# The last two gate column blocks as one group of products, with the first token half ahead

## The chip, the cores and the metric

The kernel runs on one core of a Trainium2 chip. The metric is the device time of one execution in microseconds (us); of several runs the median is taken. Engines: PE (TensorE, matmul; PEld is its weight load), DVE (VectorE), ACT (ScalarE), POOL (GpSimd), SP (SyncE, which issues nearly all transfers).

## The reference

One layer over 256 tokens of width 4096, in float32. Two branches (chunked attention and a convolution module) give `y`; then come the residual sum, a gate and a final norm. The change is in the gate and the norm.

```python
h = h + jnp.concatenate([y_a, y_c], axis=-1) @ w_out[i]
gate = jax.nn.sigmoid(rms_norm(h, ple_norm_g[i]) @ w_ple_gate[i] + b_ple_gate[i])
h = h + gate * (p[i] @ w_ple[i])
return rms_norm(h, final_g)
```

`w_ple_gate` is 4096 x 4096, `w_ple` 256 x 4096. The final norm needs the sum of squares of a whole row of `h`, so no output can be stored before the last column block is done for its tokens.

## The kernel before

**Numbers in two parts.** A matmul in full float32 is made of three in the format fp32r: each operand is split into a high part (`wh`, a cast on ACT, L197) and a low part (`wl`, the remainder, a subtraction on DVE, L198); the kinds are high x high, low x high, high x low. The tokens are two halves of 128 (`h` is 0 or 1), the 4096 output columns eight blocks of 512 (`c` is 0 to 7), the 4096 input columns 32 k-blocks of 128.

**Two ways to multiply.** `product` (matmuls at L210, in `accumulate`) takes one column block: for each k-block six matmuls of 128x512, three kinds for two token halves. `mixed_product` (matmuls at L351, in `add`) takes two column blocks at once: a pair of k-blocks, two column blocks and two token halves form a 2x2 by 2x2 block product. A plain pair is eight products, 24 matmuls. A pair with a star in the order list is done by seven products (Winograd's form of Strassen's method), 21 matmuls; for that DVE adds weight tiles (`ua`, `ub`, L398 to L403), and the sums are split as well (`uh`, `ul`). Four more PSUM banks (`P1`, `P5`, `P6`, `P7`) hold helper products, which `helper_sums` folds into the tiles `z` when the last starred pair is done.

**Order.** `units` turns a text into the order of the 16 pairs, with stars. A scheduler orders the instructions of each engine; what is marked by `pin` keeps the program's order. `later` is a queue of small steps, of which `fill` takes a few after each pair. The pool `w` has five buffers for weight tiles as loaded, `wh` and `wl` three each, `uh` and `ul` two; SP issues a load when a buffer is released.

**The gate.** `gated_pair` does the blocks 0 to 5 in three groups of two: `mixed_product` over `w_ple_gate`, then the embedding `p @ w_ple` by `product` into `pacc` (24 matmuls), then the gate: multiply-add (L978), sigmoid (L979), and by way of `later` the product with `pacc`, the sum into `hc`, the sum of squares (`square_sum`, L469) and the product with the final weight (L177).

**The last two blocks.** Blocks 6 and 7 go by `product`, one after the other; block 7 with `lag`: the last six weight tiles (of two k-blocks each) are kept, four of them in big tiles, and used for the first token half alone. So its sum is ready first: `add_gated` (L927 to L932) and `finish` (the mean at L473 and L125, the power at L126, scalings at L941 to L945, stores at L946) run for it while `rest` does the 36 matmuls of the second half. Then `add_gated` and `finish` follow for that.

```python
acc, rest = product(w_ple_gate[0], c * NB, hT, KD, lag=lag)
add_gated(c, 0, acc[0], pacc[0], row, fg)
rest()
finish(0, fg)
add_gated(c, 1, acc[1], pacc[1], row, fg)
finish(1, fg)
```

Of the kernel before, what the change touches and what calls it, by code (L numbers as in the profile page):

```python
# [10 lines left out]
F32 = mybir.dt.float32  # L11
F32R = mybir.dt.float32r
AF = mybir.ActivationFunctionType
# [3 lines left out]
P = 128  # L17
NB = 512
# [8 lines left out]
def hybrid_block(  # L27
# [107 lines left out]
    def big_tile(pool=None):  # L135
        return (pool or big).tile([P, 4, 2, T], F32R, tag="big", name="big_t")
# [64 lines left out]
        )  # L201
        return (wh, wl), made

    def accumulate(acc, h, lhs, kb, wh, wl, k, kblocks, kinds=range(3)):
        t, i = lhs[kb // 4], kb % 4
        xh = t[:, i, 0, h * P : (h + 1) * P]
        xl = t[:, i, 1, h * P : (h + 1) * P]
        for kind in kinds:
            a, b = ((xh, wh), (xl, wh), (xh, wl))[kind]
            nc.tensor.matmul(  # L210
                acc, a, b[:, k, :],
                start=kb == 0 and kind == 0, stop=kb == kblocks - 1 and kind == 2,
            )

    def product(w, col, lhs, kblocks, pool=None, tag="acc", ahead=None, lag=(), given=(), fills=2):

        acc = [
            (pool or ps_acc).tile([P, NB], F32, tag=tag, name=f"acc{h}") for h in range(NH)  # L220
        ]
        starts = list(range(len(given))) + list(range(len(given), kblocks, KC))
        kept = starts[len(starts) - len(lag) :] if lag else []
        held = []
        for k0 in starts:
            kc = 1 if k0 < len(given) else min(KC, kblocks - k0)
            if k0 < len(given):
                wh, wl = given[k0]
                for kind in range(3):
                    for h in range(NH):  # L230
                        accumulate(acc[h], h, lhs, k0, wh, wl, 0, kblocks, (kind,))
                continue
            keep = k0 in kept
            wh, wl = weight_parts(w, col, k0, kc, lag[kept.index(k0)] if keep else None)
            if keep:
                held.append((k0, kc, wh, wl))
            for k in range(kc):
                for h in range(1 if keep else NH):
                    accumulate(acc[h], h, lhs, k0 + k, wh, wl, k, kblocks)
                if ahead and given and k0 + k == len(given):  # L240
                    ahead(k0)
            if ahead:
                ahead(k0 + kc)
            fill(fills)

        def rest():
            for k0, kc, wh, wl in held:
                for k in range(kc):
                    accumulate(acc[1], 1, lhs, k0 + k, wh, wl, k, kblocks)

        return (acc, rest) if lag else acc

# [66 lines left out]
    def units(text):  # L321

        return [(int(u.rstrip("*")), u.endswith("*")) for u in text.split()]
# [3 lines left out]
    dense = units("1 0* 3 2* 5 4* 6* 7 8* 9 10* 11 12* 14* 13 15")  # L327
    delayed = units("1 3 5 7 0* 9 2* 11 4* 13 6* 15 8* 10 12 14")
    early = units("1 3 5 7 0* 9 2* 11 4* 13 6* 15 8 10 12 14")
    late = units("1 3 5 7 9 11 13 15 0* 2 4* 6 8* 10* 12 14")  # L330

    def mixed_product(
        w, col, lhs, comb, order, on_helpers, ahead=None, fills=0, on_begin=None, apart=NB
    ):

        c = [[ps_acc.tile([P, NB], F32, tag="acc", name=f"acc{h}{j}") for j in range(2)] for h in range(NH)]
        helper = {}
        begun, ends = set(), {}  # L340
        for n, (_, seven) in enumerate(order):
            for name in ("P1", "P5", "P6", "P7", "P2", "P3", "P4") if seven else ("P2", "P3", "P4", "X"):
                ends[name] = n
        banks = {"P2": c[0][0], "P3": c[0][1], "P4": c[1][0], "X": c[1][1]}
        made = []

        def add(name, x, w2, n, final):

            for kind, (a, b) in enumerate(((x[0], w2[0]), (x[1], w2[0]), (x[0], w2[1]))):
                made.append(  # L350
                    nc.tensor.matmul(  # L351
                        banks[name], a, b, start=name not in begun,
                        stop=final and ends[name] == n and kind == 2,
                    )
                )
                begun.add(name)
# [6 lines left out]
        for n, (pair, seven) in enumerate(order):  # L363
# [3 lines left out]
            for k in range(2):  # L367
                wt = wpool.tile([P, 2, NB], F32, tag="w", name="wt")
                kb = 2 * pair + k
                rows = w[kb * P : (kb + 1) * P, :]  # L370
                nc.sync.dma_start(
                    wt,
                    bass.AP(
                        tensor=rows.tensor, offset=rows.offset + col,
                        ap=[list(rows.ap[0]), [apart, 2], [1, NB]],
                    ),
                )
                wts.append(wt)
            if not seven:
                for k in range(2):  # L380
                    wh, wl = parts_of(wts[k], 2)[0]
                    for j in range(2):
                        for h in range(NH):
                            name = (("P2", "P3"), ("P4", "X"))[h][j]
                            add(name, block(2 * pair + k, h), (wh[:, j], wl[:, j]), n, k == 1)
                fill(fills)
                continue
# [39 lines left out]
            if n == last_seven:  # L427
                on_helpers(helper)
            fill(fills)
        return c  # L430

    tt, stt = nc.vector.tensor_tensor, nc.vector.scalar_tensor_tensor
    QUARTERS = ((0, 0), (1, 0), (0, 1), (1, 1))
# [30 lines left out]
            )  # L464
        return t

    def square_sum(dst, src):
        junk = spool.tile([P, NB], mybir.dt.bfloat16, tag="junk", name="junk", bufs=1)
        nc.scalar.activation(junk, src, AF.Square, accum_out=dst)  # L469

    def rstd_of(partial, n, name):
        r = cpool.tile([P, partial.shape[1]], F32, name=name)
# [447 lines left out]


    n_f = D // NB
    ssq_f = cpool.tile([P, NH, n_f], F32, name="ssq_f")

    def add_gated(c, h, acc, pacc, row, fg):
        hc, gt = hs[c][:, h, :], gts[h]
        nc.vector.scalar_tensor_tensor(gt, acc, r_h[:, h : h + 1], row, ALU.mult, ALU.add)  # L927
        nc.scalar.activation(gt, gt, AF.Sigmoid)
        nc.vector.tensor_tensor(gt, pacc, gt, ALU.mult)
        last = c == n_f - 1  # L930
        (nc.vector if last else nc.gpsimd).tensor_tensor(hc, hc, gt, ALU.add)
        square_sum(ssq_f[:, h, c : c + 1], hc)  # L932
        if not last:
            nc.gpsimd.tensor_tensor(hc, hc, fg, ALU.mult)

    def finish(h, fg):
        r = rstd_of(ssq_f[:, h : h + 1, :], D, f"r_f{h}")
        for c in range(n_f - 1, -1, -1):
            hc = hs[c][:, h, :]
            if c == n_f - 1:  # L940
                nc.vector.scalar_tensor_tensor(hc, hc, r, fg, ALU.mult, ALU.mult)  # L941
            elif c % 2:
                nc.vector.tensor_scalar(hc, hc, r, None, ALU.mult)
            else:
                nc.scalar.activation(hc, hc, AF.Identity, scale=r)  # L945
            nc.sync.dma_start(out[0, h * P : (h + 1) * P, c * NB : (c + 1) * NB], hc)  # L946

    def gated_pair(c0, order, ahead):

# [26 lines left out]
        for h, j in QUARTERS:  # L976
            gt, hc = z[h][j], hs[c0 + j][:, h, :]
            stt(gt, acc[h][j], r_h[:, h : h + 1], gt, ALU.mult, ALU.subtract if j else ALU.add)  # L978
            nc.scalar.activation(gt, gt, AF.Sigmoid)  # L979
            later.append(partial(tt, gt, pacc[j][h], gt, ALU.mult))  # L980
            todo.append(partial(tt, hc, hc, gt, ALU.add))
            todo.append(partial(square_sum, ssq_f[:, h, c0 + j : c0 + j + 1], hc))
            todo.append(partial(tt, hc, hc, fgs[j], ALU.mult))
        later.extend(todo)

    for c0 in range(0, n_f - 2, 2):
        gated_pair(c0, steady if c0 else late, None if c0 else h_ahead)

    for c in range(n_f - 2, n_f):
        row = broadcast_row(b_ple_gate, c * NB, NB)  # L990
        fg = broadcast_row(final_g, c * NB, NB)
        pacc = product(w_ple[0], c * NB, pT, PLE // P, pool=ps_tmp, tag="tmp")
        gt = spool.tile([P, NH, NB], F32, tag="stage", name="gt")
        gts = [gt[:, h, :] for h in range(NH)]
        if c < n_f - 1:
            acc = product(w_ple_gate[0], c * NB, hT, KD)
            for h in range(NH):
                add_gated(c, h, acc[h], pacc[h], row, fg)
        else:
            keep = [big_tile(more).rearrange("q a b t -> q (a b t)") for _ in range(4)]  # L1000
            lag = [
                [t[:, i * KC * NB : (i + 1) * KC * NB].rearrange("q (k n) -> q k n", n=NB) for i in range(2)]
                for t in keep
            ] + [None] * 3
            acc, rest = product(w_ple_gate[0], c * NB, hT, KD, lag=lag)
            add_gated(c, 0, acc[0], pacc[0], row, fg)
            rest()
            finish(0, fg)
            add_gated(c, 1, acc[1], pacc[1], row, fg)
            finish(1, fg)  # L1010


# [28 lines left out]
```

## Time and profile before

| | |
|---|---|
| Median of 3 runs | 2061.18 us (2059.1 to 2062.29) |
| The profiled execution's own time | 2063.82 us |
| Its span | 2061.7 us |
| Mean granted TensorE clock | 0.996 |
| PE busy | 2034.6 us (99%) |
| DVE busy | 1822.1 us (88%) |
| ACT busy | 1152.9 us (56%) |

The profile is one execution; its span goes from the first to the last instruction, and its own time lies 2.1 us above. Lines with L are lines of the kernel before. In rows of instruction groups the operands stand as out<-in. In the stretches, each engine's busy us is followed by the number of its instructions. In the timeline, a bracket tells how long the engine had been idle and what released it.

### The profile page before, as it was taken

What the parts mean: (1) busy time and instruction counts of PE and PEld (TensorE: products, weight loads), DVE (VectorE), ACT (ScalarE), POOL (GpSimd) and SP (SyncE); (2) the same over time, 40 slices, a digit from 0 to 9 for tenths busy, and PEclk for the clock granted to TensorE, in tenths of its full rate; (3) what the DMA queues carried; (4) which work ended last, traced back from release to release, by engine and by line L of the source; (5) the groups of instructions that cost most, each with busy time, mean ns of one, the idle gap of its engine ahead of it and who ended that gap; (6) DMA issues with size and microseconds to landing.
All of it is one profiled execution on the core that took longest, in us unless ns stands there. A gap on an engine that the chain in (4) does not pass through costs nothing.

```text
span 2061.7 us, 25882 instructions
## 1 busy us (share of the span) xinstructions
PE 2034.6 (99%) x9140; PEld 1675.2 (81%) x9140; DVE 1822.1 (88%) x2541; ACT 1152.9 (56%) x1479; POOL 42.9 (2%) x37
## 2 busy tenths in 40 slices
PE   9999999999999999999999999999999999999997
PEld 7888888887888787788888888878888888888886
DVE  7599999899977998875889999899999999999954
ACT  7445535554564535575556656576565666656543
POOL 0000000000000002300000000000000000000000
PEclk9999999999999999999999999999999999999998
DMA  8656665656566665555666666666666656666664
GB/s 291 186 186 201 191 197 184 195 188 188 175 204 185 194 190 164 186 184 195 194 210 202 200 215 197 212 229 206 212 202 206 211 185 192 210 229 210 220 208 166
DMA packets 170331, 412.27 MB, mean 200 GB/s; under 512 B 13006, under 2 KB 16222, under 8 KB 170202
## 3 DMA queue, kind: packets, MB, share of 16 engines
q1 hardware_dynamic: 169914, 410.11, 62.5%
q8 instruction: 71, 1.16, 0.2%
q10 hardware_dynamic: 288, 0.52, 0.1%
q14 instruction: 58, 0.48, 0.1%
HBM read 406.39 MB, written 4.19 MB: 199 GB/s over the span
## 4 chain that ended last, share of the span: by engine, by line
PE 90%; DVE 6%; issue 2%; DMA 1%; ACT 1%; POOL 0%; SPq 0%; ACTq 0%; POOLq 0%; DVEq 0%
PE acc L351 53%; PE acc L210 22%; PE acc_P L351 13%; DVE wl L198 2%; DVE cv L574 1%; PE tmp_ps L156 1%; DVE ul L198 1%; DMA wt<-in_w_in_dram 1%; DMA wt<-in_w_ple_gate_dram 0%; PE tmp_ps L724 0%; PE tmp_ps L739 0%; PE tmp_ps L757 0%; ACT wh L197 0%; DMA xin<-in_x_dram 0%; PE tmp_ps L762 0%
## 5 line engine op out<-in xcount | busy, mean ns | idle before, releaser
L197 ACT CAST wh<-wt 128x1024 fp32r<-128x1024 f32 (+1 forms) x741 | 727.0, 991 | 628.8 <-PE acc L351 319.6
L351 PE MATMUL acc<-wh,big_t 128*128 128x512 f32 x3344 | 1038.8, 391 | 3.4 <-ACT big_t L142 2.9
L198 DVE TENSOR_TENSOR wl<-wt,wh 128x1024 fp32r<-128x1024 f32 (+1 forms) x741 | 850.7, 1159 | 130.2 <-ACT wh L197 127.6
L351 PEld LDWEIGHTS acc<-wh,big_t 128*128 128x128 f32 x3344 | 626.7, 188 | 133.3 <-ACT big_t L142 3.4
L351 PE MATMUL acc<-wl,big_t 128*128 128x512 f32 x1672 | 652.1, 391 | 3.3 <-DVE wl L198 3.2
L210 PE MATMUL acc<-wh,big_t 128*128 128x512 f32 x1248 | 390.2, 393 | 0.0
L351 PEld LDWEIGHTS acc<-wl,big_t 128*128 128x128 f32 x1672 | 314.4, 188 | 71.9 <-DVE wl L198 7.2
L210 PEld LDWEIGHTS acc<-wh,big_t 128*128 128x128 f32 x1248 | 234.9, 189 | 48.2 <-DVE big_t L143 0.2
L210 PE MATMUL acc<-wl,big_t 128*128 128x512 f32 x624 | 243.4, 391 | 0.0
L574 DVE SCALAR_TENSOR_TENSOR cv<-uT,dw,cv 128x256 f32<-128x256 f32 x480 | 214.3, 487 | 1.0
L197 ACT CAST uh<-ub 128x1024 fp32r<-128x1024 f32 x103 | 108.3, 1051 | 113.1 <-DVE ub L403 92.4
L351 PE MATMUL acc_P<-uh,big_t 128*128 128x512 f32 x534 | 163.7, 390 | 0.0
L197 ACT CAST uh<-ua 128x1024 fp32r<-128x1024 f32 x103 | 108.6, 1054 | 63.9 <-DVE ua L399 59.0
L210 PEld LDWEIGHTS acc<-wl,big_t 128*128 128x128 f32 x624 | 117.9, 189 | 24.1
L198 DVE TENSOR_TENSOR ul<-ub,uh 128x1024 fp32r<-128x1024 f32 x103 | 128.2, 1245 | 7.9 <-ACT uh L197 7.1
L198 DVE TENSOR_TENSOR ul<-ua,uh 128x1024 fp32r<-128x1024 f32 x103 | 125.8, 1222 | 0.4
L351 PEld LDWEIGHTS acc_P<-uh,big_t 128*128 128x128 f32 x534 | 99.9, 188 | 21.4 <-ACT uh L197 0.8
L351 PE MATMUL acc_P<-ul,big_t 128*128 128x512 f32 x267 | 103.8, 393 | 0.9 <-DVE ul L198 0.9
L398 DVE TENSOR_TENSOR ua<-wt 128x512 f32<-128x512 f32 x103 | 71.6, 695 | 30.7 <-DMA wt<-in_w_in_dram 17.4
L399 DVE TENSOR_TENSOR ua<-wt 128x512 f32<-128x512 f32 x103 | 70.8, 688 | 4.6 <-DMA wt<-in_w_in_dram 4.3
L403 DVE TENSOR_TENSOR ub<-ub,wt 128x512 f32<-128x512 f32 x103 | 72.2, 701 | 1.2
L402 DVE TENSOR_TENSOR ub<-ua,wt 128x512 f32<-128x512 f32 x103 | 70.9, 688 | 0.2
(199 smaller groups left out, 1349.3 us busy)
## 6 DMA issues: line engine op xcount, KB each, us to landing
wt<-in_w_in_dram SPq DMA_DIRECT2D x447, 512.0 KB, 3.9
wt<-in_w_out_dram SPq DMA_DIRECT2D x128, 512.0 KB, 4.2
wt<-in_w_ple_gate_dram SPq DMA_DIRECT2D x128, 512.0 KB, 4.0
wt<-in_w_pw_dram SPq DMA_DIRECT2D x32, 512.0 KB, 4.3
hc<-in_x_dram SPq DMA_DIRECT2D x8, 512.0 KB, 5.3
wt<-in_w_ple_dram SPq DMA_DIRECT2D x8, 512.0 KB, 4.7
out_dram<-hc SPq DMA_DIRECT2D x16, 256.0 KB, 2.9
xin<-in_x_dram SPq DMA_DIRECT2D x7, 512.0 KB, 8.3
```

The lines of the kernel that those rows point to most:

```text
L156: nc.tensor.transpose(pt[:, i * T + h * P : i * T + (h + 1) * P], src[:, h, b * P : (b + 1) * P], ident,)
L197: nc.scalar.copy(wh[:, :kc, :], wt[:, :kc, :]),
L198: nc.vector.tensor_tensor(wl[:, :kc, :], wt[:, :kc, :], wh[:, :kc, :].bitcast(F32), ALU.subtract),
L210: nc.tensor.matmul(acc, a, b[:, k, :], start=kb == 0 and kind == 0, stop=kb == kblocks - 1 and kind == 2,)
L351: nc.tensor.matmul(banks[name], a, b, start=name not in begun, stop=final and ends[name] == n and kind == 2,)
L398: plus(ua[:, 0], w0[:, 0], w0[:, 1])
L399: plus(ua[:, 1], w0[:, 1], w1[:, 1])
L402: plus(ub[:, 0], ua[:, 0], w1[:, 1])
L403: plus(ub[:, 1], ub[:, 0], w1[:, 0])
L574: nc.vector.scalar_tensor_tensor(cv[:, i, :], uT[:, i, k : k + T], dw[:, b, k : k + 1], cv[:, i, :], ALU.mult, ALU.add,)
```

## The change

The blocks 6 and 7 become one group of `mixed_product`, in the order `final`: 7 of the 16 pairs are starred. The last three pairs of that order (13, 14 and 15) are left out of the group's own loop: their weight tiles are split and held (the first three in `wh` and `wl`, the last three in big tiles), and `add_left` multiplies them later, first for token half 0 in both blocks, then for half 1 in block 6, and last for half 1 in block 7, there as two halves of 256 columns in banks of their own, 36 matmuls instead of 18.

The embedding of these blocks is done after the left products of each token half (`embedded`), with `uh` and `ul` for its weight parts. The gate, the sums and the final norm are pinned in a written order. The square is scaled so that the sum of squares is the mean, `EPS` is a column of `ssq_f`, and all but the last entry are summed ahead (`sum_of`), so that one small sum (`rstd_with`) and the power stay behind the last square. The outputs of the blocks 6 and 7 are multiplied by the final weight ahead of the scaling (`weigh`). `product` loses its `lag`.

```diff
+    final = units("1 0* 3 2* 5 4* 6* 7 8* 9 10* 12* 11 13 14 15")
...
+        n_left = len(left) // 2
-        for n, (_, seven) in enumerate(order):
+        for n, (_, seven) in enumerate(order[: len(order) - n_left]):
...
+        def add_left(h, js, out=None, cols=slice(None)):
+            for m in range(0, len(held), 2):
+                for j in js:
+                    dst = c[h][j] if out is None else out[:, cols]
+                    for i, (kb, (wh, wl)) in enumerate(held[m : m + 2]):
+                        xh, xl = block(kb, h)
+                        for kind, (a, b) in enumerate(((xh, wh), (xl, wh), (xh, wl))):
+                            pin(
+                                nc.tensor.matmul(
+                                    dst, a, b[:, j, cols],
+                                    start=out is not None and m + i + kind == 0,
+                                    stop=m + i + 1 == len(held) and kind == 2,
+                                )
+                            )
...
+            if n >= len(order) - n_left:
+                for k in range(2):
+                    tiles = left[2 * (n - len(order) + n_left) + k]
+                    held.append((2 * pair + k, parts_of(wts[k], 2, tiles and tiles())[0]))
+                fill(fills)
+                continue
...
-    ssq_f = cpool.tile([P, NH, n_f], F32, name="ssq_f")
+    ssq_f = cpool.tile([P, NH, n_f + 2], F32, name="ssq_f")
+    nc.vector.memset(ssq_f[:, :, :1], EPS)
+    square_f = partial(square_sum, scale=D ** -0.5)
...
+    acc, add_left = mixed_product(
+        w_ple_gate[0], c0 * NB, hT, hS, final, on_helpers, fills=4, on_begin=on_begin,
+        left=[None] * 3 + [kept] * 3,
+    )
+    fill(len(later))
+    w_p = []
+    for j in range(2):
+        wt = wpool.tile([P, 2, NB], F32, tag="w", name="wt")
+        nc.sync.dma_start(
+            wt, w_ple[0, :, (c0 + j) * NB : (c0 + j + 1) * NB].rearrange("(k q) n -> q k n", q=P)
+        )
+        w_p.append(pair_parts(wt))
...
+    def gate(h, j, a, op, cols=slice(0, NB)):
+        gt = z[h][j][:, cols]
+        pin(stt(gt, a, r_h[:, h : h + 1], gt, ALU.mult, op))
+        pin(nc.scalar.activation(gt, gt, AF.Sigmoid))
+
+    def add_gated(h, j, pacc, at, cols=slice(0, NB)):
+        gt, hc = z[h][j][:, cols], hs[c0 + j][:, h, cols]
+        pin(tt(gt, pacc[:, cols], gt, ALU.mult))
+        pin(tt(hc, hc, gt, ALU.add))
+        pin(square_f(ssq_f[:, h, at : at + 1], hc))
+
+    def weigh(h, j, cols=slice(0, NB)):
+        pin(tt(z[h][j][:, cols], hs[c0 + j][:, h, cols], fgs[j][:, cols], ALU.mult))
...
+    def store(h, r):
+        for c in range(n_f):
+            t = hs[c][:, h, :] if c < c0 else z[h][c - c0]
+            if c % 2:
+                pin(nc.scalar.activation(t, t, AF.Identity, scale=r))
+            else:
+                pin(nc.vector.tensor_scalar(t, t, r, None, ALU.mult))
+            nc.sync.dma_start(out[0, h * P : (h + 1) * P, c * NB : (c + 1) * NB], t)
+
+    pin(stt(z[1][1], acc[1][1], r_h[:, 1:2], z[1][1], ALU.mult, ALU.subtract))
+    add_left(0, range(2))
+    gate(0, 0, acc[0][0], ALU.add)
+    gate(0, 1, acc[0][1], ALU.subtract)
+    for j in range(2):
+        add_gated(0, j, embedded(0, j), n_f - 1 + j)
+    weigh(0, 0)
+    r = rstd_with(0, sum_of(0, n_f), n_f)
+    weigh(0, 1)
+    add_left(1, [0])
+    store(0, r)
+    gate(1, 0, acc[1][0], ALU.add)
+    paccs = [embedded(1, j) for j in range(2)]
+    add_gated(1, 0, paccs[0], n_f - 1)
+    weigh(1, 0)
+    halves = [slice(i * NB // 2, (i + 1) * NB // 2) for i in range(2)]
+    parts = []
+    for cols in halves:
+        parts.append(ps_acc.tile([P, NB], F32, tag="acc", name="part"))
+        add_left(1, [1], parts[-1], cols)
+    for i, cols in enumerate(halves):
+        gate(1, 1, parts[i][:, cols], ALU.add, cols)
+        if i:
+            weigh(1, 1, halves[0])
+        add_gated(1, 1, paccs[1], n_f + i, cols)
+    s = sum_of(1, n_f + 1)
+    weigh(1, 1, halves[1])
+    store(1, rstd_with(1, s, n_f + 1))
```

## The prediction

> **What bounds the kernel now.** I read the page's busy times first, then the stretches, the chain that ended last, DVE's waits, and the timeline of the last matmuls.
>
> ```profile
> PE 2034.6 (99%) x9140; PEld 1675.2 (81%) x9140; DVE 1822.1 (88%) x2541; ACT 1152.9 (56%) x1479; POOL 42.9 (2%) x37
> ...
> core 0: us, PE busy (x) PEld busy (x) DVE busy (x) ACT busy (x) POOL busy (x), PEclk, DMA share, GB/s
> 1866.00:1890.00 24.00, 24.00 (x107) 19.74 (x106) 23.90 (x32) 14.56 (x22) 0.00 (x0) 1.00 0.59 188
> 1980.00:1990.00 10.00, 10.00 (x46) 8.29 (x45) 4.30 (x4) 4.22 (x4) 0.00 (x0) 1.00 0.59 183
> ...
> 1939.97 10.43 PE acc L351 x46
> 1950.40 88.41 PE acc L210 x390
> ```
>
> PE is full in both stretches, but they differ. At 1866 (a group by `mixed_product`) DVE has 23.9 of 24 us too; at 1980 (column block 6 by `product`) DVE has 4.3 of 10. The chain gives the pace: 46 matmuls in 10.43 us, 0.2267 us each. So fewer matmuls shorten the last part only if DVE, idle there now, can make the operands of a seven-product group in time.
>
> ```profile
> DVE ua L398 <- DMA wt<-in_w_ple_gate_dram: 2.2, 1, 2.2
> DVE z L978 <- PE acc L351: 1.3, 1, 1.3
> DVE ul L198 <- ACT uh L197: 1.2, 1, 1.2
> ...
> 1808.14 2.36 DVE L198 TENSOR_TENSOR wl<-wt,wh 128x1024 fp32r<-128x1024 f32 x2
> 1810.41 1.22 DVE L198 TENSOR_TENSOR ul<-ub,uh 128x1024 fp32r<-128x1024 f32 x1
> 1811.54 0.69 DVE L198 TENSOR_TENSOR wl<-wt,wh 128x512 fp32r<-128x512 f32 x1
> ```
>
> The first three are all that DVE waited for in the group of blocks 4 and 5 (1862 to 1950), 4.7 us. The others give its pace: 1.135 us from one 128x1024 subtraction to the next (1808.14, 1810.41, 1811.54), and 0.602 for a 128x512 one by the starts of its neighbours.
>
> ```profile
> 2047.93 0.39 PE L210 MATMUL acc<-wl,big_t 128*128 128x512 f32 x1
> 2048.35 0.75 DVE L927 SCALAR_TENSOR_TENSOR gt<-acc,r_h,row 128x512 f32<-128x512 f32 x1 [2.90 <-PE acc L210]
> 2049.14 0.63 ACT L928 ACTIVATE gt<-gt 128x512 f32<-128x512 f32 x1 [3.06 <-DVE gt L927]
> 2049.80 0.69 DVE L929 TENSOR_TENSOR gt<-acc,gt 128x512 f32<-128x512 f32 x1 [0.69 <-ACT gt L928]
> 2050.53 0.69 DVE L931 TENSOR_TENSOR hc<-hc,gt 128x512 f32<-128x512 f32 x1
> ...
> 2052.26 0.15 DVE L125 TENSOR_SCALAR r_f<-r_f 128x1 f32<-128x1 f32 x1
> 2052.49 0.56 POOL L126 TENSOR_TENSOR r_f<-r_f,mhalf 128x1 f32<-128x1 f32 x1 [9.02 <-DVE r_f L125]
> 2053.09 0.72 ACT L945 ACTIVATE hc<-hc,r_f 128x512 f32<-128x512 f32 x1 [1.05 <-POOL r_f L126]
> ```
>
> After the last matmul nothing overlaps: gate, sigmoid, product, sum, square, mean, power, 4.74 us from 2048.35 to 2053.09. The stores take the 8.6 us to the span's end.
>
> **Matmuls: −4.76 us.** Before, the two blocks are 2 x 192 gate matmuls plus 24 of the embedding, 408. After, 7 pairs x 21, 6 pairs x 24, three left pairs x 24 and 24 of the embedding are 387, counting two halves as one. 21 x 0.2267 = 4.76 us, all on the path: PE has no gap in these stretches.
>
> **Halves: 0 (0 to +4.0).** 18 matmuls of 512 columns become 36 of 256; no such row exists. The nearest by shape are plain f32 (L738, L739): their starts lie 0.108 us apart at 128 columns and 0.218 at 256, so the price follows the columns with no fixed part, and a weight load fits under 0.108. I take half of 0.2267, 36 x 0.1133. No row suggests less than half, which excludes a gain; the upper end is the full 0.2267 each, 18 x 0.2267 = 4.1. The Trainium skill's "TensorE: Matmul & The Clock Gate" (Back-to-back issue gap) gives N/2.4 + 2.5 ns, 109 ns for 256 columns, while its section LDWEIGHTS gives 107 ns to load 128 columns, which speaks against cutting further. By those figures, as an estimate, the term would be 36 x 0.109 − 4.08 = −0.15 us; no run here shows it yet.
>
> **The last chain: −1.4 us.** Four DVE and ACT steps and the square see 256 columns. DVE's 128x512 product takes 0.69 and a 128x256 one 0.42 (L681); the multiply-add goes from 0.75 to 0.48 (L143); ACT's cast goes from 0.620 to 0.405 at 256 columns (L692). So 3 x 0.27 + 2 x 0.215 = 1.24 less. Of the reduction and the scaling (0.16 and 0.15) one small sum stays behind the square, 0.2 less. Bounds −1.0 to −1.6. The first half must be through by then: it ends 2.04 us earlier, and DVE's share of it is about 1.7 us. Ahead of it on DVE stand the first token half's gates, sums and four scalings, with block 6 of the second half: about 11 us, against 11.8 from the end of the first half's products. ACT's four scalings (2.5 us) end before the sigmoid behind them is needed. If that cover is gone, the excess is paid at once; I take nothing (0 to +0.8).
>
> **Stores: −0.25 us (0 to −0.3).** The first store waited 0.75 us for a multiply-add with the final weight; now for a 0.48 scaling. The eight stores after it are bound by the transfers (some 380 GB/s in the DMA view of the last 22 us), and the first token half's eight end before them, so the rest stays.
>
> **Waiting for operands: +2.45 us (0 to +10).** I walk DVE's own order in the changed program. Its start is as after the group of blocks 2 and 3, where instructions stand alike: the four gates (L978) ended at 1864.35, 2.17 after the first embedding matmul (1862.18). The same place is now 1950.24 + 2.17 = 1952.41. From there to the low part of the fourth left weight tile (the second of pair 14, the first kept in a big tile), 37 subtractions of 128x1024, 50 steps of 128x512 and 4 multiply-adds stand in DVE's queue: 37 x 1.135 + 50 x 0.602 + 4 x 0.66 = 74.7, done at 2027.15. PE starts the group 24 matmuls after 1950.24, at 1955.68, and needs that tile behind 308 more, 69.8 us, at 2025.50. So PE is 1.65 early. DVE's real steps add about 0.55 us per 56 to such a sum (groups of blocks 2 to 5, waits for DMA left out), 0.8 in all. Behind the waiting matmul stands all of PE's queue, so it is paid in full; the later left tiles and the embedding's (short by up to 1.2 and 0.3) hide behind it. Weight loads have 2.8 us to spare or more until the last one, at 4.1 us from issue to landing. Lower end 0: DVE a few per cent faster. Upper end: the rival on ACT below.
>
> **At nothing.** The loads of `w_ple` move behind the gate's on SP, and the last `final_g` row behind them, ahead of the stores; it lands 4 us after its issue and is read some 6 us later; uncovered, the difference delays the stores. One memset joins DVE at the start, when PE waits for `x` (0 to +0.2). POOL loses four steps (5 us) that nobody waited for.
>
> Sum: −4.76 − 1.4 − 0.25 + 2.45 = −3.96, call it −4.0. The profiled execution took 2063.82 us (span 2061.7), the median of the runs is 2061.18; I take the difference off the median: 2057.2.
>
> **Rivals.**
> - No wait: DVE keeps up. For it: in the groups at 1776 and 1862 PE lost at most 0.4 us to operands, at times with 0.1 us to spare. Against: here two seven-product pairs follow each other near the end, with no later group's work to fill in. −6.4, 2054.8.
> - The halves run at the full 0.2267. Then −4.0 + 4.1: 2061.3.
> - The wait lowers PE's clock. Behind a gap of 1.94 us at 1341.4 the granted clock was 0.58 for 4 us and matmuls came every 0.43; excess 2.1 us. Against: behind a gap of 1.6 us at 808 it stayed 1.00. The largest piece of the wait here is 1.8 us. −1.9, 2059.3. The Trainium skill (same page, HAM oscillation) asks for an idle gap above about 3.4 us; by that rule this would not occur, while the row at 1341 shows that 1.94 can do.
> - Slower: ACT becomes the bound of the group. Its casts of sums stand behind weight casts that wait for PE to release a buffer; DVE waited 1.2 us for one such cast per group so far. If each of the seven pairs pays that once, DVE comes 7 x 1.2 = 8.4 later, and the sum is +4.4: 2065.6. It decides from 6.4 us of lag on; for it, two dense pairs of stars; against, ACT's 14.6 of 24 us busy.
>
> That the change does nothing is excluded: PE's order shows the 21 fewer.
>
> **How the numbers follow.** A measurement tells about 0.2% (4.1 us) from no change; that line is 2057.06, and my forecast lies on it. Forecast 0.60 (2055.8 to 2058.6), split evenly by the line; no wait 0.16, faster; halves 0.08, same; clock 0.08, same; ACT 0.08, slower. Faster 0.30 + 0.16 = 0.46, same 0.30 + 0.16 = 0.46, slower 0.08. The range goes from just below "no wait" to "halves" with their price: 2054.0 to 2061.4; it leaves out ACT and the edges.
>
> **What would show it.** After the last embedding of blocks 4 and 5, PE without gaps to about 70 us into the group, then one of 1.5 to 2.5 us that ends on DVE's low part of a kept big tile; matmuls of 256 columns every 0.113; 3.3 us from the first gate step on the last half to the power's end. Gaps on `uh` from early in the group would show ACT; a granted clock below 1 behind the gap, the third rival; a spacing of 0.2 or more, the second.

## The result, and the profile after

The changed kernel took 2067.36 us, the median of 8 runs (2065.75 to 2069.20), against 2061.31 for the kernel before (8 runs, 2059.10 to 2063.77): a ratio of 1.0027, with a 95% interval of 1.0018 to 1.0036. It is 6 us slower where 4 us less were forecast. The profiled execution took 2065.76 us, its span 2064.0, at a granted clock of 0.998.

The busy times of the page, and three stretches (the busy us of each engine, with the number of its instructions):

```profile
PE 2036.9 (99%) x9137; PEld 1668.9 (81%) x9137; DVE 1859.8 (90%) x2603; ACT 1164.1 (56%) x1497; POOL 37.4 (2%) x33
```

```profile
core 0: us, PE busy (x) PEld busy (x) DVE busy (x) ACT busy (x) POOL busy (x), PEclk, DMA share, GB/s
1866.00:1890.00 24.00, 24.00 (x105) 19.52 (x104) 24.00 (x33) 16.04 (x23) 0.00 (x0) 1.00 0.61 197
1980.00:1990.00 10.00, 10.00 (x46) 8.14 (x45) 9.62 (x13) 5.00 (x8) 0.00 (x0) 1.00 0.65 231
2030.00:2040.00 10.00, 8.62 (x39) 6.75 (x38) 10.00 (x12) 3.94 (x5) 0.00 (x0) 1.00 0.40 136
```

The change did what it says: 3 matmuls fewer in the count (21 fewer, but 18 are now two halves), and DVE, busy for 4.3 us of 1980 to 1990 before, is now busy for 9.62. But the first stretch, far ahead of the edit, has 105 matmuls where it had 107, with PE busy throughout and the clock at 1.00. The start of the embedding of blocks 4 and 5, the last place ahead of the new group, gives the sizes. In the profiled executions it came at 1950.23 us before and at 1955.42 after, 5.2 later. From there to the end of the span it took 111.42 us before and 108.56 after, 2.9 less. So the group gained, and more than that was lost ahead of it. These two executions show the loss too small: an execution of the kernel before with 256 bytes of padding, whose runs take as long as those of the kernel before (below), came to this place at 1946.73, 8.7 earlier than the changed one.

The chain of waits shows how the loss comes about. Here is the embedding of blocks 2 and 3, the same 24 matmuls with the same operands and no gap, first before, then after (start, length, what):

```profile
1862.34 5.44 PE acc L210 x24
```

```profile
1866.65 5.60 PE acc L211 x24
```

PE doesn't wait here; each matmul comes 7 ns later than it did. The groups of matmuls in the stretch from 1400 to 1950 us, ahead of the group in both kernels, show which are concerned (busy us, then mean ns of one; matmuls overlap, so that one lasts 390 ns by the profile while the next starts 227 ns after it). Before:

```profile
L351 PE MATMUL acc<-wh,big_t 128*128 128x512 f32 x1090 | 336.4, 390 | 1.2 <-ACT big_t L142 1.2
L351 PE MATMUL acc_P<-uh,big_t 128*128 128x512 f32 x222 | 67.9, 390 | 0.0
...
L351 PE MATMUL acc_P<-uh,comb_t 128*128 128x512 f32 x48 | 14.8, 389 | 0.0
L210 PE MATMUL acc<-wh,comb_t 128*128 128x512 f32 x32 | 9.9, 389 | 0.0
```

After:

```profile
L362 PE MATMUL acc<-wh,big_t 128*128 128x512 f32 x1075 | 333.0, 391 | 1.2 <-ACT big_t L142 1.2
L362 PE MATMUL acc_P<-uh,big_t 128*128 128x512 f32 x222 | 69.3, 396 | 0.0
...
L362 PE MATMUL acc_P<-uh,comb_t 128*128 128x512 f32 x48 | 15.0, 393 | 0.0
L211 PE MATMUL acc<-wh,comb_t 128*128 128x512 f32 x32 | 10.1, 396 | 0.0
```

`wh` with `big_t` is nearly as before; `uh` with `big_t` and `wh` with `comb_t` take 6 to 7 ns more, `uh` with `comb_t` 4. Measured between the starts of successive matmuls of 512 columns from 1054 to 1948 us, the mean (of spacings from 200 to 260 ns) was 226.9 ns before and 229.3 after. Over some 3,800 matmuls that is 3,800 x 2.4 ns = 9.1 us.

What the two slowest kinds share is where their operands lie. `wh`, `wl`, `big_t`, `hc` and `wt` are allotted from one end of SBUF; the second phase's `uh`, `ul`, `comb_t` and `z` are in a pool opened at the other end (`lpool`, side 1). The change adds small tiles: `ssq_f` grows from 64 to 80 bytes per partition, which takes 96 in the layout (its steps are of 32), and two sums of 32 bytes come with it. They lie in `cpool`, ahead of all pools of the first end, and so these start 96 bytes further on; the other end's stay. In the addresses of the two programs (bytes in a partition):

| | before | after |
|---|---|---|
| `hc`, `wh`, `big_t` (first tile) | 3808, 57056, 81632 | 3904, 57152, 81728 |
| the same modulo 256 | 224 | 64 |
| `uh`, `comb_t` (other end) | 212960, 188384 | 212960, 188384 |
| the same modulo 256 | 224 | 224 |

That is one theory: matmuls are slower when their two operands start at different places, by some modulus. (As it stands it leaves `uh` with `comb_t` open, which both lie at the other end; the trace answers that behind the table of placements.) Its rivals: the new tiles or the schedule slow something else, or the executions differ by themselves.

### The profile page after: what moved, and what is told of

It is laid out like the page before. It is cut to its first block, busy times and chain, and to the rows that moved or that the text cites. A ratio compares the mean times of both kernels' runs of the same rounds, so it can differ in the third digit from the quotient of the medians.

```text
span 2064.0 us, 25963 instructions
## 1 busy us (share of the span) xinstructions
PE 2036.9 (99%) x9137; PEld 1668.9 (81%) x9137; DVE 1859.8 (90%) x2603; ACT 1164.1 (56%) x1497; POOL 37.4 (2%) x33
## 4 chain that ended last, share of the span: by engine, by line
PE 88%; DVE 7%; issue 2%; DMA 2%; ACT 1%; POOL 0%; SPq 0%; ACTq 0%; POOLq 0%; DVEq 0%
PE acc L362 55%; PE acc L211 17%; PE acc_P L362 13%; DVE wl L198 3%; DMA wt<-in_w_in_dram 1%; DVE cv L591 1%; DVE ul L198 1%; PE tmp_ps L156 1%; PE tmp_ps L741 0%; PE tmp_ps L756 0%; DVE ub L420 0%; PE tmp_ps L774 0%; DVE ub L419 0%; ACT wh L197 0%; DMA wt<-in_w_ple_dram 0%
## 5 line engine op out<-in xcount | busy, mean ns | idle before, releaser
L362 PE MATMUL acc<-wh,big_t 128*128 128x512 f32 x3466 | 1078.0, 392 | 3.7 <-ACT big_t L142 2.9
L362 PEld LDWEIGHTS acc<-wh,big_t 128*128 128x128 f32 x3466 | 649.0, 188 | 142.9 <-ACT big_t L142 3.4
L362 PE MATMUL acc<-wl,big_t 128*128 128x512 f32 x1733 | 675.2, 392 | 3.4 <-DVE wl L198 3.3
L362 PEld LDWEIGHTS acc<-wl,big_t 128*128 128x128 f32 x1733 | 325.2, 188 | 74.3 <-DVE wl L198 6.4
L211 PE MATMUL acc<-wh,big_t 128*128 128x512 f32 x1024 | 320.0, 393 | 0.8 <-DVE big_t L143 0.8
L211 PEld LDWEIGHTS acc<-wh,big_t 128*128 128x128 f32 x1024 | 192.0, 189 | 40.4 <-DVE big_t L143 1.1
L211 PE MATMUL acc<-wl,big_t 128*128 128x512 f32 x512 | 199.4, 390 | 0.0
L197 ACT CAST uh<-ub 128x1024 fp32r<-128x1024 f32 x110 | 115.6, 1051 | 109.7 <-DVE ub L420 99.0
L362 PE MATMUL acc_P<-uh,big_t 128*128 128x512 f32 x570 | 176.9, 395 | 0.0
L197 ACT CAST uh<-ua 128x1024 fp32r<-128x1024 f32 x110 | 115.8, 1052 | 61.0 <-DVE ua L416 55.1
L198 DVE TENSOR_TENSOR ul<-ub,uh 128x1024 fp32r<-128x1024 f32 x110 | 136.8, 1244 | 8.9 <-ACT uh L197 8.5
L198 DVE TENSOR_TENSOR ul<-ua,uh 128x1024 fp32r<-128x1024 f32 x110 | 134.5, 1222 | 0.7
L211 PEld LDWEIGHTS acc<-wl,big_t 128*128 128x128 f32 x512 | 96.5, 188 | 19.7
L415 DVE TENSOR_TENSOR ua<-wt 128x512 f32<-128x512 f32 x110 | 76.4, 695 | 29.7 <-DMA wt<-in_w_in_dram 18.3
L416 DVE TENSOR_TENSOR ua<-wt 128x512 f32<-128x512 f32 x110 | 75.8, 689 | 4.3 <-DMA wt<-in_w_in_dram 3.9
```

Source lines behind the costliest of these rows:

```text
L197: nc.scalar.copy(wh[:, :kc, :], wt[:, :kc, :]),
L198: nc.vector.tensor_tensor(wl[:, :kc, :], wt[:, :kc, :], wh[:, :kc, :].bitcast(F32), ALU.subtract),
L211: nc.tensor.matmul(acc, a, b[:, k, :], start=kb == 0 and kind == 0, stop=kb == kblocks - 1 and kind == 2,)
L362: nc.tensor.matmul(banks[name], a, b, start=name not in begun, stop=final and ends[name] == n and kind == 2 and not (left and name in "P2 ...
L415: plus(ua[:, 0], w0[:, 0], w0[:, 1])
L416: plus(ua[:, 1], w0[:, 1], w1[:, 1])
```

## The experiments

All kernels here keep the arithmetic. A kernel is padded by widening `r_f1`, a small tile of `cpool`; no instruction changes by it. "Left" is the end of `wh` and `big_t`, "right" that of `uh` and `comb_t`. Ratios are to the kernel before in the same series, with 95% intervals.

**The changed kernel with 32 bytes of padding**, so that the ends agree modulo 128 (left 96, right 224):

```diff
-        r = cpool.tile([P, 1], F32, name=f"r_f{h}")
+        r = cpool.tile([P, 1 + (8 if h else 0)], F32, name=f"r_f{h}")[:, :1]
```

> The changed kernel, with its last small tile 32 bytes wider; no instruction is added or moved. All tiles of the pools opened after the small ones start 32 bytes further on, at 32 modulo 64 again, as in the kernel before, and as the sums' parts uh and ul of the second phase do, which are laid out from the other end. Theory place (matmuls are slower where the one operand starts at 0 and the other at 32 modulo 64): the drift of 8.3 us between 1054 and 1955 goes, the spacing is 0.2267 throughout, and the time is 2061.3 - 3 = 2058 us (2057 to 2060). Theory program (the new order or its longer code slows the parts ahead of it in some other way): unchanged, 2067 us.

Measured: 2065.40 us, ratio 1.0018 (1.0009 to 1.0027). The padding brought little, and matmuls stayed 228.9 ns apart. Agreement modulo 128 isn't enough.

**The kernel before with 96 bytes**, which puts its tiles where the change put them (left 64, right 224):

```diff
-        r = cpool.tile([P, partial.shape[1]], F32, name=name)
+        wide = 24 if name == "r_f1" else 0
+        r = cpool.tile([P, partial.shape[1] + wide], F32, name=name)[:, : partial.shape[1]]
```

> The kernel before, with its last small tile 96 bytes wider, so that every tile starts where it does in the changed kernel; no instruction is added or moved. Theory place: the second phase drifts by some 8 us as in the changed kernel, 2069 to 2071 us. Theory program: unchanged, 2061 us.

Measured: 2070.59 us, ratio 1.0042 (1.0030 to 1.0055), 8.7 us more than the kernel before in the same series. Not one instruction of the change is in this kernel, and its matmuls come 229.4 ns apart from 1054 to 1948 us, as in the changed one. So the placement alone makes a loss of this size.

**The kernel before with 64 bytes** (`wide = 16`; left 32, right 224):

> The kernel before, with its last small tile 64 bytes wider. Tiles from both ends still agree modulo 64, not modulo 128. Theory place: unchanged, 2061 us (a change of 8 us would say that 128 bytes count and not 64). Theory program: unchanged, 2061 us. It tells whether any shift at all costs time.

Measured: 2070.49 us, ratio 1.0038 (1.0025 to 1.0051). Agreement modulo 64, the first guess at the modulus, is worth nothing.

**The changed kernel with the other end moved instead**, 32 bytes down (left 64, right 192):

```diff
+    shift = pool("shift", 1, side=1).tile([P, 8], F32, name="shift")
+    nc.gpsimd.memset(shift, 0.0)
     spool = upool = pool("lpool", 2, side=1)
```

> The changed kernel, with a tile of 32 bytes (and one memset on POOL) ahead of the second phase's pool, so that uh, ul and the last combined tile start 32 bytes lower, at 0 modulo 64, as wh, wl and the big tiles do in it. Theory place, if it is the disagreement of the two operands that costs: 2058 us. If it is the start at 0 that costs: no better than 2067, or worse. Theory program: unchanged, 2067 us.

Measured: 2064.83 us, ratio 1.0011 (1.0002 to 1.0020). None of the expected times came, but the rows tell something. Here are two of the groups of 1400 to 1950 us:

```profile
L362 PE MATMUL acc_P<-uh,big_t 128*128 128x512 f32 x222 | 68.5, 392 | 0.0
L211 PE MATMUL acc<-wh,comb_t 128*128 128x512 f32 x32 | 10.0, 395 | 0.0
```

The kernel with 32 bytes of padding has 392 and 395 in these rows too, though neither end starts where the other kernel's does (64 and 192; 96 and 224). What the two share is the distance of 128. The kernel before with 96 bytes and the changed kernel, 160 apart, both have 396 in both. So the difference modulo 256 seemed to decide, and the next series tested that.

**The changed kernel with 160 bytes** (`1 + (40 if h else 0)`; both ends at 224):

> The changed kernel with its last small tile 160 bytes wider; no instruction is added or moved. Tiles from both ends now agree modulo 256 (224), as in the kernel before and in none of the first four. Theory place, with 256 for 64 (agreement modulo 64 or 128 was not enough): spacing 0.2267 throughout, no drift, 2061.9 - 3 = 2059 us (2057 to 2060). Theory any shift (only the places of the kernel before are fast, whatever the distance) and theory program: 2065 to 2067 us.

Measured: 2058.98 us, ratio 0.9985 (0.9977 to 0.9994). As the theory of agreement modulo 256 had it; the change is now a gain. The rows of 1400 to 1950 us and the chain's embedding:

```profile
L362 PE MATMUL acc_P<-uh,big_t 128*128 128x512 f32 x222 | 67.9, 390 | 0.0
L211 PE MATMUL acc<-wh,comb_t 128*128 128x512 f32 x38 | 11.7, 389 | 0.0
```

```profile
1860.19 5.44 PE acc L211 x24
```

They are back at 390, 389 and 5.44 us, and the starts at 226.9 ns.

**The kernel before with 256 bytes** (`wide = 64`; both at 224 again, though their distance modulo 512 changes):

> The kernel before with its last small tile 256 bytes wider: all tiles of the first end 256 bytes further on, those of the other end where they were; agreement modulo 256 as before. Theory place with 256: unchanged, 2062 us. Theory any shift: as with 96 and 64 bytes, 2070 us.

Measured: 2062.53 us, ratio 1.0001 (0.9992 to 1.0010): no change, 226.9 ns. Padding as such cost nothing here.

**Both ends at 64**: the changed kernel with the other end moved by 160 bytes (`[P, 40]` in place of `[P, 8]` in `shift`), otherwise the same instructions in the same order as the kernel with `[P, 8]`. (Against the changed kernel, too, PE, DVE, ACT and SP have the same operations in the same order in the programs; only POOL has the memset and its waits more.)

> The changed kernel with the second phase's pool moved down by 160 bytes instead of 32: the tiles at both ends of the memory start at 64 modulo 256 now, as in none of the kernels so far (before and the +160 one: 224 at both). Theory agreement (what counts is that the two operands of a matmul start at the same place modulo 256, not which place): matmuls 226 to 228 ns apart between 1400 and 1950 us, and the time of the +160 kernel, 2058.5 to 2060. Rival value (224 is a good place and 64 a bad one, and a pair is as slow as its worse operand): all pairs are slow, 232 ns or more, and the time is 2067 or more. Rival of the moved pool (what the pool's move of 32 bytes brought was an accident of order): 2064 to 2067, as there.

Measured: 2057.38 us, ratio 0.9977 (0.9969 to 0.9986). Its rows:

```profile
L362 PE MATMUL acc_P<-uh,big_t 128*128 128x512 f32 x222 | 67.8, 389 | 0.0
L211 PE MATMUL acc<-wh,comb_t 128*128 128x512 f32 x33 | 10.2, 389 | 0.0
```

At 64 and 64 the matmuls are as fast as at 224 and 224; at 64 and 192 or 64 and 224 they are slow. The agreement of the two ends counts, not the place. All nine placements, by the distance from left to right modulo 256:

| distance | kernels | mean spacing, 1054 to 1948 us |
|---|---|---|
| 0 | before, before + 256, changed + 160, both at 64 | 226.9 ns in each |
| 128 | changed + 32, changed with the right end at 192 | 228.9, 228.8 |
| 160 | changed, before + 96 | 229.3, 229.4 |
| 192 | before + 64 | 229.0 |

Distances other than these were not tried.

**Which matmuls are slow.** The starts of successive matmuls in the trace of the changed kernel (1054 to 1948 us) answer what the rows left open. `uh` or `ul` with `big_t` came 233.2 ns apart in the mean, `wh` or `wl` with `comb_t` 233.3, `uh` or `ul` with `comb_t` 231.3, `wh` or `wl` with `big_t` 228.1; before, all four lay between 226.7 and 227.0. The first two, whose operands lie at different ends, make some 5 us of the loss. The other two, whose operands agree, make some 4: being the most, 2,836 matmuls, `wh` and `wl` with `big_t` alone cost over 3. So a matmul can be slow though its own operands agree.

Where they are slow shows in their order. As long as PE reads from the first end alone and waits for nothing, starts are 226 or 227 ns apart. Ahead of the first `comb_t`, the matmul beside which the first weight load from `comb_t` runs is slow already, with 236 or 237 ns to the next start, in all 10 such places of the changed kernel. Ahead of `uh` with `big_t`, the matmul before is still at 226 or 227, and the first `uh` takes 234 or 235, in all 50. Behind such a passage, `wh` and `wl` with `big_t` need two to nine matmuls until they are back at 226 or 227. The same tail follows a wait where no operands disagree: in the kernel with 160 bytes, the ten matmuls behind the one that follows PE's gap of 1.6 us came 224 to 240 ns apart, then 226 or 227 again. These rows fit a reading in which whatever puts PE out of its pace costs several matmuls, and a change between ends that disagree does so each time; what happens in the chip, they don't show. That it isn't `uh` itself can be seen in the first phase of the changed kernel, where `uh` lies at the same end as `big_t`: there `uh` with `big_t` came every 227.2 ns.

**The changed kernel with 160 bytes, and the last 18 products undivided:**

```diff
-    halves = [slice(i * NB // 2, (i + 1) * NB // 2) for i in range(2)]
+    halves = [slice(0, NB)]
...
-    s = sum_of(1, n_f + 1)
-    weigh(1, 1, halves[1])
-    store(1, rstd_with(1, s, n_f + 1))
+    s = sum_of(1, n_f)
+    weigh(1, 1, halves[0])
+    store(1, rstd_with(1, s, n_f))
```

> As the changed kernel with 160 bytes, and the last left products in one piece of 512 columns (18 matmuls for 36), gate, sum and square after them in one piece too. From the trace of the changed kernel: 36 halves at 0.120 took 4.3 us, 18 at 0.2267 take 4.1, so PE ends 0.2 us earlier, and the last chain is 1.24 us longer. Theory halves pay: 1.0 us slower than with 160 bytes. Theory halves cost (their fixed part eats the chain's gain): same or faster.

Measured: 2058.61 us, ratio 0.9981 (0.9972 to 0.9990), no different from the divided one's 0.9985. In the traces the part from the embedding of blocks 4 and 5 to the end took 108.89 us against 108.03, 0.86 more, where 1.0 was expected. The runs can't show so small a difference (the medians lie the other way round); what the halves bring stands on one execution of each.

**The changed kernel with 160 bytes, and six starred pairs**, without the last one ahead of the left tiles:

```diff
-    final = units("1 0* 3 2* 5 4* 6* 7 8* 9 10* 12* 11 13 14 15")
+    final = units("1 0* 3 2* 5 4* 6* 7 8* 9 10* 12 11 13 14 15")
```

> As the changed kernel with 160 bytes, and pair 12 without its star: six pairs by seven products. Three matmuls more (0.7 us), 4.15 us less on DVE ahead of the kept tiles. Theory wait (PE's gap of 1.54 us is DVE's share of the seventh starred pair): the gap goes, 0.7 to 0.9 us faster than with 160 bytes. Theory that the gap is the kept tiles' own (their casts come late whatever stands ahead): the gap stays, 0.7 us slower.

Measured: 2057.49 us, ratio 0.9973 (0.9964 to 0.9981). The gap of 1.6 us is gone, for three matmuls more, and the last part takes 106.60 us instead of 108.03, which is 1.4 less where 0.7 to 0.9 were expected: the small pieces beside the gap shrink as well (0.94 us with seven stars, described with the next run, and 0.57 here). In the times the two intervals overlap, so the step of 1.5 us from seven stars to six rests on the trace, one execution of each. This kernel is faster than the kernel before and than the changed one as it stands, with the lowest ratio of all, though the interval of the kernel with both ends at 64 overlaps with it.

**The same with one starred pair** (`0*` alone):

> The +160 kernel with one starred pair (0*) instead of seven: 18 matmuls more, no dense DVE work ahead of the left tiles; the tail as in the changed kernel. If the group's gain is the sum of its terms: +18 x 0.2267 = +4.1, less the gaps of 1.6 and 0.2 = +2.3 against the +160 kernel (2058.98), 2061.3; against the kernel before with its 2062.5, the tail alone is then worth 1.2 to 1.5. If seven products cost something that the gaps don't show (slower matmuls beside a busy DVE): less than +1.5, below 2060.5. If fewer stars gain on as from seven to six (-1.5): below 2058.

Measured: 2059.93 us, ratio 0.9992 (0.9983 to 1.0001). The last part took 109.41 us, 1.38 more than with seven stars where 2.3 were expected. The account of that expectation had only the two gaps of 1.6 and 0.2 us; with seven stars the matmuls of this part also lose 0.94 us in pieces of under 0.12 us (the sum of all spacings above 0.2267), with one star 0.07. So 4.08 − 1.83 − 0.87 = 1.38. That is the second branch of the expectation: seven products cost something that the two gaps don't show.

## Why the prediction was wrong

**The step that failed** is one that the prediction took without saying so: that all ahead of the group stays in time as it was. It put the group's start by "The same place is now 1950.24 + 2.17 = 1952.41", from the trace of before, and its sum has no term for what lies ahead. The order of matmuls there is the same; their spacing isn't. What the prediction put at 1950.24, the start of the embedding ahead of the group, came at 1955.42, and the missing term is 9.1 us by the spacings up to 1948 us and 8.7 by the kernel before with 96 bytes. No row of the profile before could have given this price, since all its operands agree; but the wider `ssq_f` and the new sums could be seen in the diff, and the shift in the addresses of the built program. None of the rivals had it. The slower rival (ACT's casts) did not occur: DVE waited for no cast in the group, and PE's weight loads for `uh` 0.5 us in all.

**The rest of the sum can be checked** where the placement is right, in the changed kernel with 160 bytes against the kernel before with 256: from the embedding of blocks 4 and 5 to the end 108.03 against 111.44 us, −3.41, where −3.96 was forecast. These are single executions; the medians of the two, 2058.98 and 2062.53, lie 3.55 apart.

- Matmuls: −4.76 forecast. With the 24 of that embedding, 432 become 393 and 36 halves; the spacing of the whole ones outside the waits was 0.2267 as supposed. Right.
- Halves: 0 forecast, +0.23 measured. The 36 start within 4.193 us, 0.1198 apart, not 0.1133. The row of plain f32 matmuls misled: there the price followed the columns; here a piece of 256 columns takes 13 ns / 2 more than half of one of 512. The Trainium skill's formula, quoted in the prediction from "TensorE: Matmul & The Clock Gate" (Back-to-back issue gap), gives the gap of an isolated matmul, and was further off: 109 ns for 256 columns.
- The last chain: −1.4 forecast, −1.42 measured. From the start of the last matmul to the power's end it took 5.12 us before and 3.60 now; 0.11 of the difference is the shorter matmul. The timeline of the changed kernel shows it:

```profile
2051.03 1.24 PE L351 MATMUL part<-big_t 128*128 128x256 f32 x9
...
2052.31 0.48 DVE L1035 SCALAR_TENSOR_TENSOR z<-part,r_h,z 128x256 f32<-128x256 f32 x1 [0.30 <-PE part L351]
...
2052.83 0.42 ACT L1036 ACTIVATE z<-z 128x256 f32<-128x256 f32 x1 [0.21 <-DVE z L1035]
...
2054.25 0.42 ACT L486 ACTIVATE junk<-hc 128x256 bf16<-128x256 f32 x1 [1.01 <-DVE sum_f L1050]
...
2054.79 0.16 DVE L1055 TENSOR_TENSOR r_f<-ssq_f,sum_f 128x1 f32<-128x1 f32 x1 [0.18 <-ACT junk L486]
2055.03 0.55 POOL L1056 TENSOR_TENSOR r_f<-r_f,mhalf 128x1 f32<-128x1 f32 x1 [10.08 <-DVE r_f L1055]
```

  From 2052.31 to 2055.58 are 3.27 us, 3.3 forecast. DVE waited 0.30 us for the last piece, so the first half was through in time, as supposed.
- Stores: −0.25 forecast, −0.23 measured (from the power's end to the end of the span 8.61 us before, 8.38 now).
- Waiting for operands: +2.45 forecast, all in one gap; +2.77 measured, of which that gap was 1.61. The rest the forecast didn't have: 0.22 at a wait for ACT's `uh`, and 0.94 in small pieces (0.52 in six spacings of 0.27 to 0.34 us, the other 0.42 in matmuls a few ns late). By them PE came to the gap 76.25 us after the embedding's start, where 75.26 was forecast, and DVE's part let it go on at 77.86, where 77.7 was. That the sums lie so close is in part luck. The one wait that the profile of the changed kernel as it stands lists for PE in the group, and its place:

```profile
PE acc L351 <- DVE big_t L198: 1.4, 1, 1.4
```

```profile
2031.69 0.61 PE L351 MATMUL acc<-big_t 128*128 128x512 f32 x2
2033.68 0.50 PE L351 MATMUL acc<-big_t 128*128 128x512 f32 x1 [1.38 <-DVE big_t L198]
2034.02 0.63 PE L351 MATMUL acc<-wh,big_t 128*128 128x512 f32 x2
```

  It begins 76.5 us after the embedding's start, 71 into the group, and ends on DVE's low part of the first kept big tile, where it was forecast. DVE itself waited for nothing in the group that its list of waits shows. The walk through its queue had that part done 77.7 us after the embedding's start; it was done after 78.2 (2033.63).

Together −4.76 + 0.23 − 1.42 − 0.23 + 2.77 = −3.41. What was added to it in the changed kernel as it stands is some 9.1 us ahead of the group and 0.5 within it (108.56 against 108.03): +6.2, and the medians gave +6.05.

**The rivals.** No wait: the wait occurred. Halves at the full price: they cost 0.120, not 0.227. A lower clock behind the gap: the granted clock was 1.00 from 2030 to 2040, with a gap of 1.5 us in it, and none of the six profiled kernels that have this gap shows matmuls 427 ns apart behind it. That agrees with the Trainium skill's rule ("TensorE: Matmul & The Clock Gate", HAM oscillation), which asks for some 3.4. The gap at 1341 us, from which the prediction took this rival, does not agree with it: all 12 profiled executions have it, with 2.04 to 2.06 us between two starts, and in 5 of them matmuls 427 ns apart follow within 3 us, in the other 7 none. In the kernel before this cost 1.4 us against the one with 256 bytes, where it didn't happen; the prediction had 2.1.

## What to carry to other kernels

A few bytes more in a small tile can move every tile behind it, so compare the start addresses of the tiles that PE reads, before and after an edit, where they come from different ends of the memory: of the distances tried here, only 0 modulo 256 was fast. When a kernel with few idle spots gets slower, measure the spacing of matmuls ahead of the edit first; if it changed there, the edit's own worth has to be read with the placement put right. The last starred pair in front of a part without DVE slack was worth less than the wait that it caused.

## What the runs showed of the hardware

- A matmul of 512 columns in fp32r, with its weight load, came every 226.9 ns on the mean where the tiles at both ends of the memory start at the same place modulo 256 bytes, and every 228.8 to 229.4 where they don't, with single ones up to 241. The distance between the ends decided (0, 128, 160 and 192 tried), not either place. Slow were matmuls with one operand from each end, and others beside and behind them. The mechanism in the chip stays open: the trace has only the starts. The Trainium skill's "SBUF — State Buffer" (A bandwidth-pool intuition that's wrong) gives the weight load a second read port, independent of the moving operand's; whether the slowing has to do with these two reads, no run here shows.
- After a wait of 1.6 us, at a granted clock of 1.00, the second to eleventh matmul still came 224 to 240 ns apart before the 226 to 227 returned (kernel with 160 bytes).
- In the first phase, from 100 to 950 us, the same mean was 227.2 to 227.3 ns in all these kernels, however they were padded: there the operands lie at one end and move together.
- Two matmuls of 256 columns took 13 ns more than one of 512 (2 x 0.1198 against 0.2267 us).
